# Beta folded into the decay matrix of a gated DeltaNet, and two row scalings issued on ScalarE

## The chip, the core and the metric

The kernel runs on one NeuronCore of one Trainium2 chip. TensorE (PE) does matmuls and transposes, VectorE (DVE), ScalarE (ACT) and GpSimd (POOL) do everything elementwise, SyncE (SP) issues the DMAs. Each engine works through its own queue in the order in which the program was laid out, and waits on semaphores for the others. The metric is the device time of one execution, in microseconds (us), as the median of several runs.

## The reference

One layer of a hybrid encoder on 1024 tokens of width 1024: RMSNorm, an input projection, a causal pooling group and a gated DeltaNet group (4 heads of width 128), an output projection, a squared-ReLU MLP of width 4096 and a last RMSNorm. The change touches the gated DeltaNet only. Its chunked form, cut to what matters here:

```python
qh = l2_norm(heads(q)) * (Dh ** -0.5)
kh = l2_norm(heads(k))
beta = per_head(jax.nn.sigmoid(b.astype(f32)))
gcum = jnp.cumsum(per_head(g), axis=-1)
diff = gcum[..., :, None] - gcum[..., None, :]
decay_incl = jnp.exp(jnp.where(incl, diff, -jnp.inf))
decay_strict = jnp.where(strict, decay_incl, 0.0)
kb = kh * beta[..., None]
m = jnp.einsum('bhncd,bhnjd->bhncj', kb, kh) * decay_strict
sol = lax.linalg.triangular_solve(jnp.eye(C) + m, rhs, left_side=True, lower=True)
attn_inner = jnp.einsum('bhncd,bhnjd->bhncj', qh, kh) * decay_incl
...
o = o * lax.rsqrt(jnp.mean(o * o, axis=-1, keepdims=True) + EPS) * gdn_norm
```

## The kernel before

The program is one straight line of instructions for a sequence cut into two halves of 512 tokens. The kernel works on DeltaNet chunks of 128 tokens, so there are eight chunks (c = 0 to 7), four to a half, and all four heads of a chunk lie side by side in one tile of 128 partitions by 4 x 128 columns.

**Two kinds of work are interleaved on PE.** The dense work is the generator `dense` (L801): the input projections k, q, v, z, p of half 0, then k, q, v, p, z of half 1, then the output projection. Every dense product is three matmuls of 128x512 (a high and a low part of each operand, in the 32-bit replicated format), so every weight tile is first split by ACT (`A.copy(hi, raw)`, L132) and then by DVE or POOL (L133). Between the dense matmuls run the strands: `prepares`, `queries`, `inverts`, `corrects`, `scans` (L692 to L724), each a loop over the eight chunks that waits for flags of the others.

**The order on PE is written out by hand.** A class `Clocked` adds up a nominal time for every matmul, a strand that yields a number sleeps for so much of that nominal time (`SLACK` is 2.0 us, `KHOP` 8.0 us), and `run` weaves the strands into the dense matmuls by it. The diff changes no matmul, no transpose and no yield, and the nominal time counts matmuls and yields alone. The order of ACT, DVE and POOL is not written by hand: the framework's scheduler lays it out with its own estimate of the times, and may pull an instruction ahead as soon as its inputs and its buffer are free in that estimate.

**One chunk**, in the order of its data:

- `prepare` (L515): ACT writes `rh` and `rl`, the triangle `upto` times the high and low part of the gate, a head at a time (L521, four instructions each). PE forms their cumulative differences in `pd`, and the chunk's transposed keys in `pk`. ACT takes `dec = Exp(pd)` (L529), POOL masks it with `upto` (L530) and subtracts the identity to get `ds` (L532). ACT squares `pk` with a sum per row (`squares`, L507, line 510), DVE adds the epsilon (L535), POOL raises to the power -0.5 (`rsqrt`, L152), and DVE scales the keys with that, `kn` (L538). PE transposes `kn`, ACT copies the result to `knT` (L543), POOL makes `kd` (L545), PE multiplies keys by keys into `pm`, and DVE forms `m` from `pm`, `beta` and `ds` in four instructions, one a head (L551). `m` is split into two half-precision tiles `m1`, `m2` (L553 to L555).
- `query` (L559): PE multiplies keys by queries into `pa`, DVE forms `at` from `pa`, `beta` and `dec` in four instructions (L571).
- `invert` (L578): six levels of products on PE. In each, DVE makes `xx` (L595), and ACT copies the two results to `t` and `tt` (L601, L602); the next level's matmuls need all three. `correct` (L608) refines the inverse; DVE makes `ee` (L617) and `hh` (L622) there.
- `scan` (L639): the state recurrence. At its end ACT squares the output, DVE adds, POOL takes the power -0.5 of `so`, and DVE scales the output, `on` (L682). PE transposes `on`, ACT scales it into `qT` (L687), and POOL gates it with `zT` (`gate_out`, L759) for the output projection.

The strand that prepares chunk c+1 starts when chunk c is queried and chunk c-1 scanned, so that preparing, inverting and scanning of neighbouring chunks overlap. Beside the strands DVE carries the causal convolution of q, k, v (three `cy` instructions a tile, L396), the running sums of the pooling group (`nxt`, L414 and L415) and part of the weight splits; ACT carries the copies out of PSUM for both.

Constants (`ident`, `upto`, `low_t`, the level masks) are made once near the start (L229 to L267). `gt` (L493) gives a tile from the pool `gp`, under a name and with a number of buffers; the tiles `rh` and `ds` share one buffer.

Of the kernel before, what the change touches and what calls it, by code (L numbers as in the profile page):

```python
# [8 lines left out]
F32 = mybir.dt.float32  # L9
F32R = mybir.dt.float32r  # L10
F16 = mybir.dt.float16
AF = mybir.ActivationFunctionType
ALU = mybir.AluOpType
PSUM = bass.MemoryType.PSUM

P = 128
# [5 lines left out]
NH = 4  # L22
# [6 lines left out]
def hybrid_trunk(ctx, tc, x, norm_mix, w_in, conv_w, w_pool, pool_scale, a_log, dt_bias,  # L29
                 gdn_norm, w_out, norm_mlp, w_up, w_down, norm_final, out):  # L30
    nc = tc.nc
    V, A, G, T = nc.vector, nc.scalar, nc.gpsimd, nc.tensor
# [23 lines left out]
    def opened(**kw):  # L56
        c = tc.tile_pool(**kw)
        return c, c.__enter__()
# [28 lines left out]
    ident = const.tile([P, P], F32, name="ident")  # L87
# [6 lines left out]
    gpc, gp = opened(name="gp", bufs=1, side="right")  # L94
# [20 lines left out]
    def work_bank():  # L115
        return psg.tile([P, HALF], F32, name="bank", tag="bank")
# [33 lines left out]
    def rsqrt(s):  # L150
        n = s.shape[-1]
        last["rsqrt"] = G.tensor_tensor(s, s, mhalf[:, :n], op=ALU.pow)  # L152
# [90 lines left out]

    upto = gp.tile([P, P], F32, name="upto")
    V.tensor_tensor(upto, ones_f, low_t, op=ALU.subtract)
    upto_r = gp.tile([P, P], F32R, name="upto_r")
    V.tensor_copy(upto_r, upto)

# [2 lines left out]
    for l in range(7):  # L251
        b = 1 << l
        m = gp.tile([P, P], F16, name=f"lev{l}")
# [30 lines left out]
    def done(name, after=0.0):  # L284
        flags[name] = T.now + after
# [198 lines left out]
    def bc(m):  # L484
        return m.unsqueeze(1).broadcast_to(hs)

    def bcol(m):
        return m.unsqueeze(2).broadcast_to(hs)

    def flat(m):  # L490
        return m.rearrange("p h c -> p (h c)")

    def gt(nm, bufs=1, dt=F32, shape=hs, tag=None):  # L493
        return gp.tile(shape, dt, name=nm, tag=tag or nm, bufs=bufs)

    def bank():
        return work_bank().rearrange("p (h c) -> p h c", h=NH)

    def mm(acc, lhsT, rhs, start=True, stop=True):
        for h in range(NH):  # L500
            T.matmul(acc[:, h, :], lhsT[:, h, :], rhs[:, h, :], start=start, stop=stop)

    def tr(acc, src):
        for h in range(NH):
            T.transpose(acc[:, h, :], src[:, h, :], ident)

    def squares(src, acc):  # L507
        junk = gt("junk", dt=F16, shape=[P, P])
        for h in range(NH):
            A.activation(junk, src[:, h, :], AF.Square, accum_out=acc[:, h:h + 1])  # L510

    def of_half(m, c):
        return m[c // CH][:, :, (c % CH) * P:(c % CH + 1) * P]

    def prepare(c, r):  # L515

        g_hi, g_lo, beta, kds, egl, eg, neg = (m[:, c % CH, :] for m in gts[c // CH])
        rh, rl = gt("rh", dt=F32R), gt("rl", dt=F32R)
        for dst, gg in ((rh, g_hi), (rl, g_lo)):
            for h in range(NH):  # L520
                A.activation(dst[:, h, :], upto, AF.Copy, scale=gg[:, h:h + 1].bitcast(F32))  # L521
        yield 2.0 * SLACK
        pd, pk = bank(), bank()
        T.matmul(pd, u_r, flat(rh), start=True, stop=False)
        T.matmul(pd, u_r, flat(rl), start=False, stop=True)
        tr(pk, of_half(kT, c))

        dec = gt("dec")
        A.activation(dec, pd, AF.Exp)  # L529
        G.tensor_tensor(dec, dec, bc(upto), op=ALU.mult)  # L530
        ds = gt("ds", tag="rh")
        G.tensor_tensor(ds, dec, bc(ident), op=ALU.subtract)  # L532
        rk = gt("rk", 2, shape=[P, NH])
        squares(pk, rk)
        V.tensor_scalar(rk, rk, 4 * EPS, None, op0=ALU.add)  # L535
        rsqrt(rk)
        kn = gt("kn")
        V.tensor_tensor(kn, pk, bcol(rk), op=ALU.mult)  # L538
        yield KHOP
        pn = bank()  # L540
        tr(pn, kn)
        knT = gt("knT", 2)
        A.copy(knT, pn)  # L543
        kd = gt("kd", 2)
        G.tensor_tensor(kd, kn, bcol(kds), op=ALU.mult)  # L545
        yield 1.2 * SLACK
        pm = bank()
        mm(pm, knT, knT)
        m = gt("m")
        for h in range(NH):  # L550
            V.scalar_tensor_tensor(m[:, h, :], pm[:, h, :], beta[:, h:h + 1], ds[:, h, :], op0=ALU.mult, op1=ALU.mult)  # L551
        m1, m2 = gt("m1", 2, F16), gt("m2", 2, F16)
        V.tensor_copy(m1, m)  # L553
        G.tensor_tensor(m2, m, m1, op=ALU.subtract)
        V.tensor_tensor(m1, m1, bc(ident_h), op=ALU.add)  # L555
        r.update(m1=m1, m2=m2, kd=kd, egl=egl, beta=beta, knT=knT, dec=dec, eg=eg, neg=neg)
        done(f"prepared{c}", 2.5 * SLACK)

    def query(c, r):  # L559

        qc = of_half(qT, c)
        sq = gt("sq")
        A.activation(sq, qc, AF.Square)
        yield 1.0 * SLACK
        pa, ps = bank(), work_bank()
        mm(pa, r["knT"], qc)
        for h in range(NH):
            T.matmul(ps[:, h:h + 1], sq[:, h, :], ones_c, start=True, stop=True)
        at = gt("at", 2)
        for h in range(NH):  # L570
            V.scalar_tensor_tensor(at[:, h, :], pa[:, h, :], r["beta"][:, h:h + 1], r["dec"][:, h, :], op0=ALU.mult,  # L571
                                   op1=ALU.mult)
        qe = gt("qe", 3, shape=[P, NH])
        V.tensor_scalar(qe, ps[:, 0:NH], 4 * EPS, EPS * P, op0=ALU.add, op1=ALU.mult)
        r.update(qe=qe, at=at)
        done(f"queried{c}")
# [62 lines left out]
    def scan(c, r):  # L639
        old = state[0]  # L640
        w = r["v"]
        if old is not None:
            pw = bank()
            mm(pw, r["knT"], old)
            w = gt("w")
            for h in range(NH):
                V.scalar_tensor_tensor(w[:, h, :], pw[:, h, :], r["neg"][:, h:h + 1], r["v"][:, h, :], op0=ALU.mult,
                                       op1=ALU.add)
            yield 1.2 * SLACK
        py = bank()  # L650
        mm(py, r["ti"], w)
        y = gt("y")
        A.copy(y, py)
        yield 1.0 * SLACK
        if c < NT - 1:
            pst = bank()
            mm(pst, r["kd"], y)
            new = gt("s", 2)
            if old is None:
                V.tensor_copy(new, pst)  # L660
            else:
                for h in range(NH):
                    V.scalar_tensor_tensor(new[:, h, :], old[:, h, :], r["egl"][:, h:h + 1], pst[:, h, :], op0=ALU.mult,
                                           op1=ALU.add)
            state[0] = new
        po = bank()
        mm(po, r["at"], y)
        if old is not None:

            pq, on = bank(), gt("on", tag="w")  # L670
            mm(pq, of_half(qT, c), old)
            A.copy(on, po)
            for h in range(NH):
                V.scalar_tensor_tensor(on[:, h, :], pq[:, h, :], r["eg"][:, h:h + 1], on[:, h, :], op0=ALU.mult,
                                       op1=ALU.add)
            po = on
        so = gt("so", shape=[P, NH])
        squares(po, so)
        V.scalar_tensor_tensor(so, so, 1.0 / P, r["qe"], op0=ALU.mult, op1=ALU.add)
        rsqrt(so)  # L680
        on = po if old is not None else gt("on", tag="w")
        V.tensor_tensor(on, po, bcol(so), op=ALU.mult)  # L682
        done(f"scan{c}", 1.0)
        yield 4.0 * SLACK
        pt = bank()
        tr(pt, on)
        A.activation(of_half(qT, c), pt, AF.Copy, scale=gnorm)  # L687
        done(f"o{c}", 1.5)
# [3 lines left out]
    def prepares():  # L692
        for c in range(NT):
            if c % CH == 0:
                yield f"k{c // CH}"
                yield f"gates{c // CH}"
            if c:
                yield f"queried{c - 1}"
            if c > 1:
                yield f"scan{c - 2}"  # L700
            yield from prepare(c, made[c])

    def queries():
        for c in range(NT):
            yield f"prepared{c}"
            if c % CH == 0:
                yield f"q{c // CH}"
            yield from query(c, made[c])
# [11 lines left out]
    def scans():  # L720
        for c in range(NT):
            yield f"corrected{c}"
            yield f"queried{c}"
            yield from scan(c, made[c])  # L724
# [133 lines left out]
    ub = [P, 4, HALF]  # L858
# [332 lines left out]
```

## Time and profile before

| what | value |
|---|---|
| median of 3 runs | 1155.54 us (1153.03 to 1156.3) |
| time of the profiled execution | 1154.56 us |
| its span, first to last instruction | 1152.9 us |
| mean granted PE clock in the span | 0.987 |

The span is 1.66 us shorter than the time of its own execution; the rest lies around it. Before about 60 us the kernel loads and normalizes the first half and projects its first keys. From there to about 475 us projections and DeltaNet chunks share the engines. After that the MLP runs, in which none of the changed lines occurs. A row of a group reads: line, engine, operation, out<-in, shapes, count, then busy time in us and mean duration of one in ns, then the idle time of that engine just before these instructions and what ended it.

### The profile page before, as it was taken

Reading aid. Unit: us, or ns where it says so; the run is one execution under the profiler, and the core shown is the slowest. Engines: PE = TensorE matmul, PEld = TensorE weight load, DVE = VectorE, ACT = ScalarE, POOL = GpSimd, SP = SyncE. Lnnn points to the kernel's source line nnn. Section 1 sums busy time; section 2 is a strip of 40 time slices with the busy share of each in tenths; the row PEclk is TensorE's granted clock in tenths of the full one; section 3 lists DMA queues with packets and bytes.
Section 4 is the critical chain, followed back from the end, with each engine's and each line's share of the span. In section 5 each row is a group of like instructions: output and inputs, shape, how many; then the busy total and the mean of one; then the engine's idle time right before and its main releaser. Section 6 shows DMA issues by size and latency. Waiting matters only on the chain.

```text
span 1152.9 us, 15516 instructions
## 1 busy us (share of the span) xinstructions
PE 1094.7 (95%) x5606; PEld 890.2 (77%) x5606; DVE 760.5 (66%) x1216; ACT 601.5 (52%) x1117; POOL 267.3 (23%) x247
## 2 busy tenths in 40 slices
PE   6999999989999899977999999999899999999997
PEld 5787887768778788755788888888778888888886
DVE  5797598777887665679655555555455687466584
ACT  6667566666566363654554545454443343334353
POOL 7023144264451200054222222222000000000010
PEclk9999999999999899997999999999989999999999
DMA  5233211111223221130544343434397896365561
GB/s 163 83 111 110 74 53 50 46 55 47 71 64 130 73 84 54 33 104 2 192 145 156 137 164 130 172 122 144 108 389 264 300 380 210 108 194 191 193 209 73
DMA packets 93047, 155.23 MB, mean 135 GB/s; under 512 B 7781, under 2 KB 45738, under 8 KB 92970
## 3 DMA queue, kind: packets, MB, share of 16 engines
q1 hardware_dynamic: 92970, 154.24, 39.6%
q8 instruction: 44, 0.72, 0.3%
q14 instruction: 33, 0.27, 0.1%
HBM read 120.66 MB, written 33.55 MB: 134 GB/s over the span
## 4 chain that ended last, share of the span: by engine, by line
PE 73%; DVE 9%; ACT 3%; POOL 2%; issue 2%; DMA 1%; POOLq 0%; DVEq 0%; SPq 0%; ACTq 0%
PE bank L44 54%; PE acc L44 18%; DVE cy L396 2%; DVE tl L930 1%; PE bank L48 1%; POOL rk L152 1%; DVE xx L595 0%; DMA x<-hd 0%; ACT th L172 0%; DVE r L921 0%; POOL wl L133 0%; DVE nxt L415 0%; DVE wl L936 0%; DVE m L551 0%; POOL wu L955 0%
## 5 line engine op out<-in xcount | busy, mean ns | idle before, releaser
L44 PE MATMUL bank<-th,wh 128*128 128x512 f32 x448 | 178.2, 398 | 11.5 <-ACT th L929 10.5
L44 PE MATMUL bank<-tl,wh 128*128 128x512 f32 x448 | 178.1, 397 | 2.5 <-DVE tl L930 2.4
L44 PE MATMUL bank<-th,wl 128*128 128x512 f32 x448 | 177.6, 396 | 2.2 <-DVE wl L936 2.2
L935 ACT CAST sh<-x 128x1024 fp32r<-128x1024 f32 x55 | 57.9, 1054 | 159.9 <-PE bank L44 153.8
L44 PE MATMUL bank<-th,sh 128*128 128x512 f32 x344 | 133.8, 389 | 0.0
L44 PE MATMUL bank<-th,sl 128*128 128x512 f32 x344 | 133.8, 389 | 0.0
L44 PE MATMUL bank<-tl,sh 128*128 128x512 f32 x344 | 133.8, 389 | 0.0
L44 PE MATMUL acc<-uh,wh 128*128 128x512 f32 x320 | 129.7, 405 | 1.6 <-DVE ul L173 0.9
L935 ACT CAST wh<-wu 128x512 fp32r<-128x512 f32 x112 | 69.1, 620 | 115.4 <-PE bank L44 97.8
L44 PE MATMUL acc<-ul,wh 128*128 128x512 f32 x320 | 128.5, 402 | 0.0
L44 PE MATMUL acc<-uh,wl 128*128 128x512 f32 x320 | 128.1, 400 | 0.0
L936 DVE TENSOR_TENSOR sl<-x,sh 128x1024 fp32r<-128x1024 f32 x55 | 67.3, 1223 | 87.5 <-ACT sh L935 87.5
L936 DVE TENSOR_TENSOR wl<-wu,wh 128x512 fp32r<-128x512 f32 x112 | 81.3, 729 | 45.0 <-ACT wh L935 45.0
L44 PEld LDWEIGHTS bank<-th,wh 128*128 128x128 f32 x448 | 85.1, 190 | 31.8 <-ACT th L929 11.2
L44 PEld LDWEIGHTS bank<-tl,wh 128*128 128x128 f32 x448 | 84.9, 190 | 24.3 <-DVE tl L930 5.2
L44 PEld LDWEIGHTS bank<-th,wl 128*128 128x128 f32 x448 | 85.1, 190 | 22.3 <-DVE wl L936 3.1
L133 POOL TENSOR_TENSOR wl<-raw,wh 128x512 fp32r<-128x512 f32 x48 | 66.9, 1397 | 93.0 <-ACT wh L132 88.7
L152 POOL TENSOR_TENSOR stf<-stf,mhalf 128x1 f32<-128x1 f32 x8 | 7.9, 998 | 329.1 <-DVE stf L1128 329.1
L44 PEld LDWEIGHTS bank<-th,sl 128*128 128x128 f32 x344 | 64.6, 188 | 13.5
L44 PEld LDWEIGHTS bank<-tl,sh 128*128 128x128 f32 x344 | 64.6, 188 | 13.5
L44 PEld LDWEIGHTS bank<-th,sh 128*128 128x128 f32 x344 | 64.5, 188 | 13.3
L44 PEld LDWEIGHTS acc<-uh,wh 128*128 128x128 f32 x320 | 60.3, 188 | 13.6 <-ACT cy L394 1.9
(322 smaller groups left out, 2290.2 us busy)
## 6 DMA issues: line engine op xcount, KB each, us to landing
w<-in_w_down_dram SPq DMA_DIRECT2D x72, 512.0 KB, 6.3
x<-hd SPq DMA_DIRECT2D x56, 512.0 KB, 3.3
raw<-in_w_in_dram SPq DMA_DIRECT2D x80, 256.0 KB, 2.7
wu<-in_w_up_dram SPq DMA_DIRECT2D x16, 1024.0 KB, 5.4
hd<-s SPq DMA_DIRECT2D x48, 256.0 KB, 2.0
hd<-u SPq DMA_DIRECT2D x32, 256.0 KB, 2.1
raw<-in_w_out_dram SPq DMA_DIRECT2D x24, 256.0 KB, 2.5
xin<-in_x_dram SPq DMA_DIRECT2D x8, 512.0 KB, 4.9
```

Source lines behind the costliest of these rows:

```text
L44: T0.matmul(out, lhsT, rhs, start=start, stop=stop, skip_group_check=goes_on)
L48: T0.transpose(out, in_, identity)
L133: eng.tensor_tensor(lo, raw, hi.bitcast(F32), op=ALU.subtract)
L152: last["rsqrt"] = G.tensor_tensor(s, s, mhalf[:, :n], op=ALU.pow)
L396: V.scalar_tensor_tensor(cy, cr[:, e:e + HALF], tap[e], cy, op0=ALU.mult, op1=ALU.add)
L930: V.tensor_tensor(TL[i][:, j, :], block(r, j), TH[i][:, j, :].bitcast(F32), op=ALU.subtract)
L935: A.copy(hi, src)
L936: V.tensor_tensor(lo, src, hi.bitcast(F32), op=ALU.subtract)
```

## The change

The DeltaNet's `beta` is multiplied into the decay matrix itself. For this ACT writes a third tile `ub`, the triangle `upto` times `beta`, a head at a time like `rh` and `rl`. POOL multiplies `dec` by `ub` where it multiplied it by `upto`, and gets `ds` by multiplying with a new constant `above` (the triangle without its diagonal, made once by DVE) where it subtracted the identity. `m` and `at` then need no `beta`: each is one DVE instruction over all heads where it was four. And the two scalings by a row's reciprocal norm, `kn` and `on`, move from DVE (one instruction over all heads) to ACT (four, one a head).

```diff
     V.tensor_tensor(upto, ones_f, low_t, op=ALU.subtract)
+    above = gp.tile([P, P], F32, name="above")
+    V.tensor_tensor(above, upto, ident, op=ALU.subtract)
...
         rh, rl = gt("rh", dt=F32R), gt("rl", dt=F32R)
-        for dst, gg in ((rh, g_hi), (rl, g_lo)):
+        ub = gt("ub")
+        for dst, gg in ((rh, g_hi), (rl, g_lo), (ub, beta)):
             for h in range(NH):
-                A.activation(dst[:, h, :], upto, AF.Copy, scale=gg[:, h:h + 1].bitcast(F32))
+                sc = gg[:, h:h + 1]
+                A.activation(dst[:, h, :], upto, AF.Copy, scale=sc if dst is ub else sc.bitcast(F32))
...
         A.activation(dec, pd, AF.Exp)
-        G.tensor_tensor(dec, dec, bc(upto), op=ALU.mult)
+        G.tensor_tensor(dec, dec, ub, op=ALU.mult)
         ds = gt("ds", tag="rh")
-        G.tensor_tensor(ds, dec, bc(ident), op=ALU.subtract)
+        G.tensor_tensor(ds, dec, bc(above), op=ALU.mult)
...
         kn = gt("kn")
-        V.tensor_tensor(kn, pk, bcol(rk), op=ALU.mult)
+        for h in range(NH):
+            A.activation(kn[:, h, :], pk[:, h, :], AF.Copy, scale=rk[:, h:h + 1])
...
         m = gt("m")
-        for h in range(NH):
-            V.scalar_tensor_tensor(m[:, h, :], pm[:, h, :], beta[:, h:h + 1], ds[:, h, :], op0=ALU.mult, op1=ALU.mult)
+        V.tensor_tensor(m, pm, ds, op=ALU.mult)
...
         at = gt("at", 2)
-        for h in range(NH):
-            V.scalar_tensor_tensor(at[:, h, :], pa[:, h, :], r["beta"][:, h:h + 1], r["dec"][:, h, :], op0=ALU.mult,
-                                   op1=ALU.mult)
+        V.tensor_tensor(at, pa, r["dec"], op=ALU.mult)
...
         on = po if old is not None else gt("on", tag="w")
-        V.tensor_tensor(on, po, bcol(so), op=ALU.mult)
+        for h in range(NH):
+            A.activation(on[:, h, :], po[:, h, :], AF.Copy, scale=so[:, h:h + 1])
```

More of the change, by code (lines that the diff above doesn't have):

```diff
@@ L555, in prepare @@
         V.tensor_tensor(m1, m1, bc(ident_h), op=ALU.add)
-        r.update(m1=m1, m2=m2, kd=kd, egl=egl, beta=beta, knT=knT, dec=dec, eg=eg, neg=neg)
+        r.update(m1=m1, m2=m2, kd=kd, egl=egl, knT=knT, dec=dec, eg=eg, neg=neg)
         done(f"prepared{c}", 2.5 * SLACK)
```

## The prediction

> **What bounds the kernel now.** I read first the page, then the busy times in stretches, then PE's waits.
>
> ```profile
> PE 1094.7 (95%) x5606; PEld 890.2 (77%) x5606; DVE 760.5 (66%) x1216; ACT 601.5 (52%) x1117; POOL 267.3 (23%) x247
> ```
>
> PE is busy for 95% of the span. The change touches no PE instruction, so all it can do is to shorten or lengthen PE's waits, and only where chunks are worked on:
>
> ```profile
> 60.00:384.00 324.00, 308.12 (x2031) 250.11 (x2030) 254.98 (x508) 210.92 (x495) 126.69 (x95) 1.00 0.26 76
> ...
> 375.00:400.00 25.00, 21.97 (x123) 16.60 (x122) 16.66 (x27) 9.77 (x22) 7.53 (x6) 0.86 0.23 79
> ```
>
> The columns after the length are PE, PEld, DVE, ACT and POOL busy time, then the granted clock. In the 324 us of the chunks PE idles 324 - 308.1 = 15.9 us; that is the whole prize. DVE is busy 255.0/324 = 79%, ACT 210.9/324 = 65%. The second row has the one place in there where the clock was held back: (1 - 0.86) x 25 = 3.5 us. Who ends PE's waits in the same 324 us (total, times, longest):
>
> ```profile
> PE bank L44 <- DVE xx L595: 3.3, 6, 0.8
> PE acc L44 <- DVE wol L133: 3.0, 2, 1.9
> PE bank L48 <- DVE kn L538: 2.7, 2, 1.4
> PE bank L44 <- DVE ee L617: 1.6, 2, 0.9
> ...
> PE bank L44 <- ACT qT L397: 1.5, 1, 1.5
> ```
>
> DVE ends most of them. So it looks right to take work off DVE; but the 2.7 us for `kn` end on an operation that the change makes longer.
>
> **The change part by part.** First the prices:
>
> ```profile
> L551 DVE SCALAR_TENSOR_TENSOR m<-bank,beta,ds 128x128 f32<-128x128 f32 x32 | 9.1, 343 | 1.7 <-PE bank L44 1.7
> ...
> L521 ACT ACTIVATE rl<-upto,g_lo 128x128 fp32r<-128x128 f32 x28 | 9.0, 405 | 0.0
> L682 DVE TENSOR_TENSOR on<-on,so 128x512 f32<-128x512 f32 x7 | 7.0, 1001 | 4.2 <-POOL so L152 4.1
> L538 DVE TENSOR_TENSOR kn<-bank,rk 128x512 f32<-128x512 f32 x8 | 5.5, 691 | 7.7 <-POOL rk L152 7.6
> ...
> L571 DVE SCALAR_TENSOR_TENSOR at<-bank,beta,dec 128x128 f32<-128x128 f32 x32 | 9.0, 342 | 2.2 <-PE bank L44 2.2
> ```
> ```profile
> 251.12 1.13 DVE L551 SCALAR_TENSOR_TENSOR m<-bank,beta,ds 128x128 f32<-128x128 f32 x4 [1.18 <-PE bank L44]
> ```
> ```profile
> 280.69 1.28 ACT L521 ACTIVATE rl<-upto,g_lo 128x128 fp32r<-128x128 f32 x4
> ```
>
> Small instructions overlap in their queue: four of `m` take 1.13 us, not 4 x 0.343. One over all heads, with one operand in PSUM, has the price of `kn`, 0.69. So **`m` and `at`** give DVE 0.44 us each a chunk, not the 0.68 that the means suggest. **`kn` and `on`** give 0.69 each. Per chunk 2.26, in eight chunks 18 us, or 5 to 6 points of DVE's 79%. DVE also stood idle 7.6 us ahead of `kn` and 4.1 us ahead of `on`, waiting for POOL's power with other work queued behind; these waits move to ACT.
>
> ACT gets three groups of four a chunk (**`ub`, `kn`, `on`**), 1.28 each by the row of `rl`, which has the same form: a 128x128 tile with a scale from a column. That is 3.84 a chunk, 31 us in all, and ACT goes from 65% to about 74%. Reading PSUM as `kn` does could be cheaper or dearer; I keep 1.28.
>
> POOL's two products keep their shape and I take their price as unchanged. `ub` must be there before POOL multiplies, and its one buffer is free again only when POOL is done with the chunk before; it is needed a chunk later, so it costs ACT time only. The constant `above` has the price of `upto`, a DVE instruction of the same shape that runs once:
>
> ```profile
> L245 DVE TENSOR_TENSOR upto<-ones_f,low_t x1: 391/391/391, 26.3 to 26.3; 128x128 f32<-128x128 f32 x1
> ```
>
> It costs 0 to 0.39 us; I take 0, since PE then has a full projection queued. Neither SP's queue nor a DMA is touched.
>
> **What PE gains.** A wait shrinks where DVE ran without a pause from a removed instruction up to the one that PE waited for.
>
> ```profile
> 332.70 0.69 DVE L538 TENSOR_TENSOR kn<-bank,rk 128x512 f32<-128x512 f32 x1 [0.90 <-POOL rk L152]
> ```
> ```profile
> 336.75 0.38 PE L44 MATMUL bank<-xx,tt 128*128 128x128 f16 x4 [0.42 <-DVE xx L595]
> ...
> 343.08 0.38 PE L44 MATMUL bank<-xx,tt 128*128 128x128 f16 x4 [0.81 <-DVE xx L595]
> ```
>
> From 332.70 to the second `xx` DVE works without a pause. Without `kn` it starts 0.90 + 0.69 = 1.59 us earlier, more than both waits: 0.42 + 0.81 = **1.23**.
>
> ```profile
> 233.43 0.69 DVE L682 TENSOR_TENSOR on<-on,so 128x512 f32<-128x512 f32 x1 [1.12 <-POOL so L152]
> ```
> ```profile
> 232.22 0.69 ACT L394 ACTIVATE cy<-acc,cols 128x512 f32<-128x512 f32 x1
> ```
> ```profile
> 238.82 0.38 PE L44 MATMUL bank<-xx,tt 128*128 128x128 f16 x4 [1.49 <-ACT qT L397]
> ```
>
> The convolution behind `on` starts as that ends, at 234.1 less the overlap of the queue; its input left ACT at 232.91. It can go about 1.1 us earlier, and `xx` and `qT` with it: **1.1** of the 1.49.
>
> ```profile
> 146.09 0.69 DVE L538 TENSOR_TENSOR kn<-bank,rk 128x512 f32<-128x512 f32 x1
> ```
> ```profile
> 149.56 0.38 PE L44 MATMUL bank<-xx,tt 128*128 128x128 f16 x4 [0.39 <-DVE xx L595]
> ...
> 87.13 0.38 PE L44 MATMUL bank<-xx,tt 128*128 128x128 f16 x4 [0.84 <-DVE xx L595]
> ...
> 304.28 0.40 PE L44 MATMUL bank<-tt,ee 128*128 128x128 f16 x4 [0.79 <-DVE ee L617]
> ```
>
> The first lies behind a `kn`: **0.39**. The other two lie behind `at` and `m`, with 0.44 to gain: **0.88**. Sum of the gains 1.23 + 1.1 + 0.39 + 0.88 = 3.6.
>
> **What PE loses.**
>
> ```profile
> 245.89 0.69 DVE L538 TENSOR_TENSOR kn<-bank,rk 128x512 f32<-128x512 f32 x1 [0.69 <-POOL rk L152]
> ```
> ```profile
> 246.07 0.58 ACT L601 CAST t<-bank 128x512 f16<-128x512 f32 x1
> 246.54 0.59 ACT L602 CAST tt<-bank 128x512 f16<-128x512 f32 x1
> ```
> ```profile
> 246.73 0.41 PE L48 MATMUL bank<-ident,kn 128*128 128x128 f32 x2 [1.45 <-DVE kn L538]
> ...
> 291.63 0.41 PE L48 MATMUL bank<-ident,kn 128*128 128x128 f32 x2 [1.28 <-DVE kn L538]
> ```
>
> In chunk 4 ACT is free for `kn` at 246.07 at the earliest, so it ends at 247.35 in place of 246.58 (0.8 later); behind `t` and `tt` it ends at 248.3 (1.75 later). I take **1.2**. In chunk 5 it is late by 1.28 - 0.69 = **0.6**. The other six `kn` and seven `on` had no wait of PE behind them.
>
> ```profile
> 281.03 1.77 DVE L682 TENSOR_TENSOR on<-on,so 128x512 f32<-128x512 f32 x1
> ```
> ```profile
> 282.95 0.30 PE L48 MATMUL bank<-ident,on 128*128 128x128 f32 x1 [0.41 <-DVE on L682]
> ```
>
> Here `on` would stand behind the four `rl` above (280.69 + 1.28 = 281.97) and end at 283.25 in place of 282.80, **0.5** later; ahead of them it would be 0.4 earlier. I keep the order of the trace.
>
> ```profile
> 369.82 0.62 ACT L132 CAST wh<-raw 128x512 fp32r<-128x512 f32 x1 [0.60 <-PE acc L44]
> 370.92 0.59 ACT L601 CAST t<-bank 128x512 f16<-128x512 f32 x1 [0.48 <-PE bank L44]
> ```
>
> An `on` of 1.28 at 369.4 fills the rest of the first gap (0.4) and the second (0.48); ACT, busy without a pause after that, is **0.4** late, and with it the split weights that PE waits for at 380.5. Last, the copies `t` and `tt` of the inversion, in the same queue, can be caught behind a group that waits for POOL. Such a hit costs the group, 1.28, and the mean wait for POOL, (7.6 + 4.1)/16 = 0.73, less the slack of the copy:
>
> ```profile
> 252.88 0.61 ACT L602 CAST tt<-bank 128x512 f16<-128x512 f32 x1
> ```
> ```profile
> 254.20 0.62 PE L44 MATMUL bank<-t,m 128*128 128x128 f16 x8
> ```
>
> 254.20 - 253.49 = 0.71, so 1.3 a hit. How often it happens the trace of before can't show, since the order of ACT is laid out anew: from none to sixteen. I count one hit, **1.3**, because PE waited for a `kn` or an `on` only three times in sixteen, so these groups mostly fall where PE has other work queued. Sum of the losses 1.2 + 0.6 + 0.5 + 0.4 + 1.3 = 4.0.
>
> **Sum.** +4.0 - 3.6 = +0.4 us on the profiled execution: 1154.56 + 0.4 = 1154.9. That execution was 1.0 below the median of 1155.54, so for the median I say **1155.9 us**: no change. What a measurement can tell here is about 0.3%, 3.5 us.
>
> [...] If all sixteen moved groups lay in PE's way, 16 x 0.59 would make it 1155.5 + 9.4 = 1164.9; the waits show three of sixteen that do.
>
> **Rivals.**
>
> *ACT becomes the queue that holds PE* (slower). `kn` and `on` sit in ACT's queue at their place and wait there for POOL's power; behind them `t` and `tt` are held, which PE needs at every level of the inversion. At 1.3 a hit it decides from four hits on, three more than I count (1155.9 + 3.9 = 1159.8); six give 1155.9 + 6.5 = **1162.4**. For it: the waits ahead of `kn` were seen on DVE, six times in eight. Against it: ACT pauses for 324 - 210.9 = 113 us of the stretch, so most groups find it free. [...]
>
> *The splits at 375 to 383 come free* (faster).
>
> ```profile
> 375.27 3.44 POOL L759 TENSOR_TENSOR qT<-qT,zT 128x512 f32<-128x512 f32 x2
> ```
> ```profile
> 377.48 2.38 DVE L767 TENSOR_TENSOR ml<-pT,mh 128x512 fp32r<-128x512 f32 x2
> ```
> ```profile
> 380.51 0.50 PE L44 MATMUL acc<-wol,mh 128*128 128x512 f32 x1 [1.93 <-DVE wol L133]
> ```
>
> DVE's `ml` lasts until POOL's gating ends, the third `wol` waits behind it, and the clock is held back just after. If the new order of the queues parts these, both waits (3.0) and the clock's loss (3.5) go: 1155.9 - 6.5 = **1149.4**. For it: the scheduler lays out all three queues anew. Against it: no changed instruction stands between them, and ACT feeds them later, not earlier. [...]
>
> *DVE's relief reaches PE more often than the trace shows*: `xx`, `ee` and `qT` together are 6.4 us, of which I count 3.6. Alone this gives 1155.9 - 2.8 = 1153.1, inside my forecast's band.
>
> **How the numbers follow.** No change 0.52; ACT holds PE 0.24; the splits come free, or DVE's relief adds to part of it, 0.24. The range goes from 1148.0 (a little below the second rival) to 1162.4 (the first); about one in ten is left out on either side. Faster by over 0.3% 0.24, within it 0.52, slower 0.24.
>
> **What would show it.** In the profile after: four ACT instructions of `kn` that take about 1.28 together; DVE near 73% and ACT near 74% in the stretch of the chunks; no wait of PE at the two `xx` after 336; PE's waits on `kn` grown from 2.7 to about 4.5 and under ACT's name; at most one or two on `t` more than before. I am wrong if PE's idle time there differs by more than 3.5 us from 15.9, or if the clock's loss near 380 is gone.

## The result, and the profile after

| kernel | median, us | runs | ratio to before (95% interval) |
|---|---|---|---|
| before | 1155.92 | 4 | |
| after | 1163.16 (1162.8 to 1164.28) | 4 | 1.0069 (1.0051 to 1.0088) |

The change makes the kernel 7.2 us slower. The forecast was no change, 1155.9, and the range ended at 1162.4. The nearest rival was "ACT becomes the queue that holds PE", by its time and by its engine; its mechanism was another one. The four runs of the changed kernel had a mean granted clock of 0.980 to 0.983, and the 81 runs of the kernel before that the experiments are compared with 0.984 to 0.988 (one run of 3859 us is left out of the ratios).

The first part of the page after, and the busy times in stretches (columns as before: PE, PEld, DVE, ACT, POOL, granted clock):

```profile
PE 1102.0 (95%) x5606; PEld 894.7 (77%) x5606; DVE 741.8 (64%) x1153; ACT 626.5 (54%) x1213; POOL 263.9 (23%) x247
```
```profile
60.00:384.00 324.00, 310.03 (x2018) 251.21 (x2017) 232.52 (x443) 228.56 (x569) 120.91 (x93) 0.98 0.25 74
375.00:400.00 25.00, 21.92 (x123) 16.70 (x122) 14.82 (x20) 15.14 (x40) 9.21 (x8) 0.86 0.32 106
```

The work moved much as was said: DVE lost 760.5 - 741.8 = 18.7 us (18 forecast) and stands at 72% in the chunks, ACT got 25 us (31 forecast) and stands at 70.5%. PE even idles less in the 324 us: 14.0 us where it was 15.9. But it also did less: 2018 matmuls where there were 2031, at a clock of 0.98 where it was 1.00. So the loss is not idle time of PE alone, and the view that the prediction watched for it (idle off by 3.5 us) does not see it. Who ended PE's waits between 60 and 480 us (total, times, longest):

```profile
PE bank L48 <- ACT kn L544: 6.8, 4, 3.0
PE acc L44 <- DVE wol L133: 3.0, 2, 1.9
PE bank L44 <- ACT t L604: 2.6, 4, 1.1
PE bank L44 <- DVE xx L598: 1.4, 4, 0.5
```

`xx` fell from 3.3 to 1.4, as hoped. `kn` rose from 2.7 to 6.8, and the two long ones are these, in chunk 4 and in chunk 6:

```profile
247.98 1.25 PE L48 MATMUL bank<-ident,kn 128*128 128x128 f32 x4 [2.69 <-ACT kn L544]
```
```profile
340.62 1.25 PE L48 MATMUL bank<-ident,kn 128*128 128x128 f32 x4 [2.99 <-ACT kn L544]
```

The order of PE's instructions is the same in both kernels, so the start of the same instruction can be compared between the two traces. At 236 us of the trace of before PE is 0.3 us late, at 240 it is 1.3 early, at 256 2.8 late (chunk 4: +4.1), from 291 to 335 1.7 late, at 352 5.9 late (chunk 6: +4.1); from there to 480 it stays (6.2), and the MLP adds 2.3 more. Each of the two steps is larger than the wait that stands in it, 1.23 and 2.99 us more than before. Most of the rest is the clock. The stretches around the two waits, two for chunk 4 and three for chunk 6:

```profile
244.33:247.74 3.41, 0.90 (x9) 0.58 (x8) 2.12 (x5) 2.19 (x5) 2.51 (x3) 1.00 0.54 151
247.74:251.16 3.42, 3.18 (x9) 2.47 (x10) 0.00 (x0) 1.55 (x5) 1.41 (x2) 0.50 0.27 77
...
336.49:339.91 3.42, 1.14 (x5) 0.58 (x4) 3.42 (x8) 1.23 (x4) 2.65 (x2) 1.00 0.47 118
339.91:343.32 3.41, 2.70 (x14) 2.32 (x15) 3.03 (x6) 2.56 (x7) 1.33 (x2) 0.50 0.10 36
343.32:346.73 3.41, 3.41 (x9) 2.38 (x8) 0.00 (x0) 0.76 (x2) 0.61 (x1) 0.50 0.01 2
```

Behind the wait in chunk 4 PE runs 3.4 us at half clock, behind that in chunk 6 6.8 us; by the starts of the same matmuls 1.6 and 2.4 us are lost in them. Not all of that is the clock: PE starts the four transposes of `kn` 0.26 us apart there, as ACT hands over the heads one by one, where they were 0.11 apart, and that is about 0.5 us in each chunk; the same step costs 0.5 us in chunk 5, at full clock. The trace of before has no such spell between 60 and 381 us.

**Why `kn` came late.** ACT around chunk 6, before:

```profile
328.43 0.28 ACT L510 ACTIVATE junk<-bank 128x128 f16<-128x128 f32 x1
328.59 0.21 ACT L510 ACTIVATION_READ_ACCUMULATOR junk<-bank 128x1 f32 x1
328.83 0.28 ACT L510 ACTIVATE junk<-bank 128x128 f16<-128x128 f32 x1
...
329.23 0.28 ACT L510 ACTIVATE junk<-bank 128x128 f16<-128x128 f32 x1
...
329.63 0.28 ACT L510 ACTIVATE junk<-bank 128x128 f16<-128x128 f32 x1
```

and after:

```profile
331.36 0.27 ACT L512 ACTIVATE junk<-bank 128x128 f16<-128x128 f32 x1
...
332.64 0.30 ACT L512 ACTIVATE junk<-bank 128x128 f16<-128x128 f32 x1
...
332.91 1.29 ACT L525 ACTIVATE ub<-upto,beta 128x128 f32<-128x128 f32 x4
334.08 0.63 ACT L132 CAST wh<-raw 128x512 fp32r<-128x512 f32 x1
334.59 0.61 ACT L604 CAST t<-bank 128x512 f16<-128x512 f32 x1
335.06 0.61 ACT L605 CAST tt<-bank 128x512 f16<-128x512 f32 x1
335.54 0.32 ACT L512 ACTIVATE junk<-bank 128x128 f16<-128x128 f32 x1
...
336.79 0.33 ACT L512 ACTIVATE junk<-bank 128x128 f16<-128x128 f32 x1
...
340.20 1.14 ACT L544 ACTIVATE kn<-bank,rk 128x128 f32<-128x128 f32 x4 [2.47 <-POOL rk L152]
```

The four squares that give the norm of the keys used to go out 0.40 us apart. Now they are spread over 5.4 us, with the new `ub` and other work between them. They all write the one buffer `junk`, which nobody reads; each waits for the one ahead of it to be out of it (in the kernel before, the second starts at 328.83 and the read of the first sum ends at 328.80), and in its place the scheduler puts whatever of ACT is ready. The last square of chunk 6 starts 2.95 us behind the transposes into `pk` before, and 8.36 behind them after; DVE's epsilon, POOL's power and `kn` follow it. ACT itself stood idle 2.47 us for that power.

Chunk 4 is a mixed case. Its squares were spread over 6.6 us already before (235.93 to 242.52), and the last one starts 9.29 us behind the transposes in place of 8.29. And there `kn` does stand behind `t` and `tt` in ACT's queue, as the prediction had it; the power was done at 246.88:

```profile
245.87 1.01 POOL L152 TENSOR_TENSOR rk<-rk,mhalf 128x4 f32<-128x4 f32 x1 [0.90 <-DVE rk L540]
```
```profile
247.07 0.59 ACT L605 CAST tt<-bank 128x512 f16<-128x512 f32 x1
247.55 1.16 ACT L544 ACTIVATE kn<-bank,rk 128x128 f32<-128x128 f32 x4
```

### The profile page after: what moved, and what is told of

It is laid out like the page before. It is cut to its first block, busy times and chain, and to the rows that moved or that the text cites. A ratio compares the mean times of both kernels' runs of the same rounds, so it can differ in the third digit from the quotient of the medians.

```text
span 1161.3 us, 15546 instructions
## 1 busy us (share of the span) xinstructions
PE 1102.0 (95%) x5606; PEld 894.7 (77%) x5606; DVE 741.8 (64%) x1153; ACT 626.5 (54%) x1213; POOL 263.9 (23%) x247
## 4 chain that ended last, share of the span: by engine, by line
PE 73%; DVE 7%; ACT 6%; issue 2%; POOL 1%; DMA 1%; POOLq 0%; DVEq 0%; SPq 0%; ACTq 0%
PE bank L44 54%; PE acc L44 18%; DVE cy L398 2%; PE bank L48 1%; DVE tl L934 1%; ACT wh L132 0%; DMA x<-hd 0%; ACT t L604 0%; ACT th L172 0%; DVE r L925 0%; ACT junk L512 0%; ACT on L686 0%; ACT rl L525 0%; DVE wol L133 0%; DVE nxt L417 0%
## 5 line engine op out<-in xcount | busy, mean ns | idle before, releaser
L398 DVE SCALAR_TENSOR_TENSOR cy<-cr,cols,cy 128x512 f32<-128x512 f32 x72 | 66.5, 928 | 10.7 <-ACT cy L396 10.0
```

The source lines that it names most:

```text
L398: V.scalar_tensor_tensor(cy, cr[:, e:e + HALF], tap[e], cy, op0=ALU.mult, op1=ALU.add)
```

## The experiments

Three theories. **S**: the added groups on ACT spread the squares over the one `junk` buffer; the power, and so `kn`, is late. **K** (the prediction's own account of chunk 4): `kn` is late because its own scaling now stands in ACT's queue. **L**: ACT simply has too much to do. All ratios are to runs of the kernel before on the same chip, with 95% intervals.

**Which part loses.** Four kernels put parts of the change back.

e1: the changed kernel with `kn` on DVE again.

```diff
-        for h in range(NH):
-            A.activation(kn[:, h, :], pk[:, h, :], AF.Copy, scale=rk[:, h:h + 1])
+        V.tensor_tensor(kn, pk, bcol(rk), op=ALU.mult)
```

> The changed kernel with kn scaled by DVE again; ub, on, m and at stay changed. Theory S (the added ACT groups ub and on stand among the squares of pk, so the power rk comes late, whoever scales kn): the last square stays 1 to 5 us later after the transposes of pk than before (it was 2.0 to 8.3 us before, 3.2 to 9.3 after), PE still waits 4 us or more for kn, and the time stays at 1160 to 1165 us. Theory K (the scaling of kn in ACT's queue is itself the loss): the waits on kn go back to 2.7 us or less, the time to 1153 to 1157 us.

Measured: 1161.73 us, 1.0048 (1.0034 to 1.0063). Most of the loss stays, and so do PE's waits, now under DVE's name:

```profile
PE bank L48 <- DVE kn L543: 8.5, 5, 3.4
```

K falls as the main cause: the squares of chunk 6 are as late as in the changed kernel (8.35 us behind the transposes), and PE's wait there is 3.4 us in place of 3.0. In chunk 4 the wait is 2.46 us in place of 2.69; so little hung on ACT's queue ahead of `kn`.

e2: the changed kernel with `on` on DVE again (the same edit in `scan`). e3: both again on DVE, so that only the folded `beta` is left. e4: the other way round, the kernel before with `kn` and `on` on ACT and no fold.

> The changed kernel with on scaled by DVE again; ub and kn stay on ACT. Theory S: one of the two groups that stand among or ahead of the squares is gone, so about half of the loss of 7 us goes: 1157 to 1161 us, the last square about 1.3 us earlier than in the changed kernel where on stood ahead of it. Theory K: no change, 1161 to 1165 us.

> Only the fold of beta (ub on ACT, m and at one instruction each); kn and on on DVE as before. Theory S: ub alone among the squares, a part of the loss stays: 1156 to 1161 us. Theory K: no loss, and DVE's relief of 0.9 us a chunk shows: 1152 to 1156 us.

> The kernel before with kn and on scaled by ACT; no ub, beta stays in m and at. Theory S: on alone ahead of the squares, about half of the loss: 1157 to 1161 us. Theory K: the whole loss, 1161 to 1165 us, with PE waiting 6 us or more for kn.

| | median, us | ratio | last square of chunk 6 behind `pk`, us | wait for `kn` there, us |
|---|---|---|---|---|
| e2 | 1158.83 | 1.0027 (1.0017 to 1.0036) | 5.49 | 1.06 |
| e3 | 1161.37 | 1.0044 (1.0028 to 1.0059) | 5.44 | 3.33 |
| e4 | 1165.37 | 1.0084 (1.0070 to 1.0098) | 7.46 | 3.97 |

e2 came out where S expected it, e3 0.4 us above. e4 did not: its time lies just above the range of K, and its waits for `kn` of 7.3 us in all are what K expected. But its trace does not show K's mechanism in chunk 6, where `kn` starts 0.03 us behind the power. There DVE, busy with the pooling group's `nxt`, gives the epsilon only 3.6 us behind the start of the last square (0.4 in the kernel before, 1.8 in the changed one). That adds to the late squares and is not part of S.

No part is innocent: each of them that adds groups to ACT moves the squares of chunk 6 from 2.95 to 5.4 us or more. But the squares are not all of it. In e2 and e3 the power of chunk 6 ends at 337.10 and 337.21 us, and `kn` starts at 337.13 on ACT and at 339.16 on DVE, behind a `nxt` of the pooling group: 2 us of e3's wait are DVE's queue, and there the scaling on ACT is the better one. The parts do not add up either: 0.44% for the fold and 0.84% for the scalings, 0.69% for both. The order of the queues is laid out anew in each kernel.

**Taking the cause away.** e5: the changed kernel, with four buffers for the squares' output. No work is removed.

```diff
-        junk = gt("junk", dt=F16, shape=[P, P])
         for h in range(NH):
+            junk = gt("junk", 4, F16, [P, P])
             A.activation(junk, src[:, h, :], AF.Square, accum_out=acc[:, h:h + 1])
```

> The changed kernel with four buffers for junk, the tile that the squares write and nobody reads. With one buffer each square must wait for the one ahead of it, and the scheduler puts one other ACT instruction or group (t, wh, ub, on) between any two; with four the squares of a chunk stand together in ACT's queue. Nothing else is changed and no work is taken away. Theory S (the gaps between the squares fill with the added ACT groups, so the power and kn come late): the last square comes within 4 us of the transposes in every chunk (3.2 to 9.3 us in the changed kernel), PE's waits on kn fall from 6.8 to under 1.5 us, the half-clock spells near 248 and 340 us are gone, and the time falls to 1150 to 1156 us. Theory L (31 us more ACT work cost what they cost, in whatever order): 1160 to 1165 us.

Measured: 1156.18 us, 1.0008 (0.9999 to 1.0017). The squares of chunk 6 in its timeline are together again, and closer than before, 0.25 us apart:

```profile
326.93 0.26 ACT L512 ACTIVATE junk<-bank 128x128 f16<-128x128 f32 x1
...
327.18 0.27 ACT L512 ACTIVATE junk<-bank 128x128 f16<-128x128 f32 x1
...
327.43 0.28 ACT L512 ACTIVATE junk<-bank 128x128 f16<-128x128 f32 x1
...
327.68 0.29 ACT L512 ACTIVATE junk<-bank 128x128 f16<-128x128 f32 x1
```

No wait for `kn` is left in the list of PE's waits, and no spell at half clock before 379 us. In the stretch from 60 to 384 us ACT is busy 230.5 us, not less than the 228.6 of the changed kernel. The time is 0.2 us above the range that S gave. So S holds for the changed kernel and L falls: 7.0 of the 7.2 us hang on one buffer.

Does the change then gain? At 377 us of the trace of before PE is 2.8 us ahead in e5. That is no proof of the prediction's gains, since e6 below has a lead of 2.4 us at 324 us without the change (e5 2.7). e5 loses its lead between 377 and 383, where the fourth weight split `wol` comes no earlier than it did:

```profile
PE acc L44 <- DVE wol L133: 4.9, 3, 2.8
```

e6: the kernel before with the same four buffers. e8: the fold alone (e3) with them. e9: the moved scalings alone (e4) with them.

> The kernel before with four buffers for junk. Theory S: it had two late kn of its own (chunks 4 and 5, 2.7 us of PE waits), which go: 1151 to 1155 us. Theory L: no change, 1154 to 1157 us.

> The fold of beta alone (ub on ACT; kn and on on DVE) with four buffers for junk. Theory S: the loss of 5 us that the fold alone showed goes and DVE's relief is left: 1150 to 1155 us. Theory L: 1158 to 1162 us, as with one buffer.

> kn and on on ACT, no fold, with four buffers for junk (with one buffer it took 1165.4 us, the worst of all). Theory S: the squares stand together, the waits on kn go, 1152 to 1157 us. Theory L (ACT's load): 1162 to 1166 us.

Measured: e6 1156.67 us, 1.0006 (0.9997 to 1.0015); e8 1156.81, 1.0008 (0.9998 to 1.0017). Both are above the ranges of S (e6 in that of L) and have no wait for `kn`. e6 gives its lead back at two others; e8 has no lead at 324 us:

```profile
PE bank L44 <- DVE xx L595: 5.3, 5, 2.5
...
PE bank L44 <- DVE nxt L414: 1.8, 1, 1.8
```

e9 was a miss: 1163.73, 1.0050 (1.0033 to 1.0067), where S alone would have it near before. Its waits for `kn` are gone too, but PE waits 2.0 us for `ee`, 1.8 for `nxt` and 5.0 for `wol`, and its clock is half in four places between 180 and 396 us. So S does not explain the loss of the moved scalings alone, and what they displace there is not shown.

e7: the changed kernel with a longer nominal sleep between `kn` and its transposes, to give the late power time.

```diff
-KHOP = 8.0
+KHOP = 11.0
```

> The changed kernel with KHOP 11.0 in place of 8.0: PE's order has 3 us more of other work between the transposes of pk and those of kn. Theory S: PE's waits on kn fall from 6.8 to under 2 us and most of the loss goes, 1153 to 1158 us, though every chunk is strung out by 3 us. Theory L: 1160 to 1165 us.

A miss for S: 1161.34, 1.0045 (1.0032 to 1.0058), which is in the range of L. The wait for `kn` fell to 0.4 us as S said, but each chunk ends later and the inversions now wait, so the run does not decide between the two:

```profile
PE bank L44 <- DVE xx L598: 8.9, 7, 1.9
```

**The place near 380.** The third `wol` (a weight split on DVE) waits for two `ml` of the output projection that are pulled ahead of it; the first runs beside POOL's gating and takes 1.77 us there, the second starts behind it and takes 0.68. e10 puts them behind it, in the changed kernel with four buffers; e11 does so in the kernel before, e12 in e6, e14 in the changed kernel with its one buffer.

```diff
-        eng.tensor_tensor(lo, raw, hi.bitcast(F32), op=ALU.subtract)
+        last["split"] = eng.tensor_tensor(lo, raw, hi.bitcast(F32), op=ALU.subtract)
...
         wt[0] += wout_weights(0, range(4, KT))
+        last["lows"] = last["split"]
...
-    parts = out_split(NT - 1)
+    with tc.issue_after(last["lows"].ins):
+        parts = out_split(NT - 1)
...
-    whole(out_proj(4, 0, wt[0], work_bank))
+    with tc.issue_after(last["lows"].ins):
+        early = out_split(4)
+    whole(out_proj(4, 0, wt[0], work_bank, early))
```

> The changed kernel with four buffers for junk and, besides, the three splits ml of later tokens (tiles 7 and 4) laid behind the four splits wol on DVE, which PE waits for near 375 to 383 us; they stood among them and were held there by POOL's gating. With four buffers alone PE was 2.7 us ahead of the kernel before at 374 us and lost it there. Expected: PE's waits on wol fall from 4.9 to under 1 us and the half-clock spell that follows goes, 1148 to 1152 us. Rival: the weights come late for another reason (ACT's split or the load), no change, 1155 to 1158 us.

> The kernel before with the same order on DVE for wol and ml alone. Expected: the wait of 3.0 us for wol and up to 3.4 us of the clock's loss go, 1149 to 1153 us. Rival: no change, 1154 to 1157 us.

> The kernel before with both (four buffers for junk, the order of wol and ml): the fair comparison for the changed kernel with both. If the change itself is worth something once its two side effects are taken away, this is slower than the changed kernel with both by 1 to 4 us; if the change is worth nothing, the two are within 1 us.

> The changed kernel with its one junk buffer, and the two split parts of the output projection issued on DVE behind the weight splits. That order took 1155.92 - 1149.9 = 6.0 us off the kernel before and 1156.18 - 1150.39 = 5.8 off the changed kernel with four junk buffers. If the late squares of chunks 4 and 6 and the third weight split are two losses that add up: 1163.16 - 5.9 = 1157.3, with the spells at half clock behind kn of chunks 4 and 6 still there and the one near 387 shorter or gone. If they are one loss (the lead lost at 340 decides what is late at 380): 1150 to 1152.

| | median, us | ratio |
|---|---|---|
| e10 | 1150.39 | 0.9952 (0.9940 to 0.9964) |
| e11 | 1149.90 | 0.9947 (0.9935 to 0.9959) |
| e12 | 1152.76 | 0.9970 (0.9959 to 0.9981) |
| e14 | 1160.38 | 1.0031 (1.0017 to 1.0046) |

In e11 the list of PE's waits up to 480 us is that of before to a tenth of a us but for this row (3.0 before), and no spell at half clock is left in that stretch:

```profile
PE acc L44 <- DVE wol L133: 1.8, 2, 1.1
```

That is 6.0 us for the order of a few instructions. At the place itself, between 377 and 390 us, PE gains 3.8 us: 1.2 of the wait and 2.6 of the clock. The profile of e11 gains another 1.9 in the MLP, where the reordered instructions are long past. In e10 the waits for `wol` fell to 2.6 us and not to under 1, and a spell of 3.4 us is left where 6.8 were. Both e10 and e11 beat both kernels, and e11 does it without the change. e10 and e12, which differ by the change alone, are 2.4 us apart, with intervals that just overlap; so much it may be worth once its side effect and this place are out of the way. e12 is 2.9 us behind e11, so the four buffers are no gain in the kernel before. e14 lies above both of its expectations: the loss in the chunks stays, and the order gives 2.8 us by the medians in place of 5.9 (by the ratios 4.4, since the kernel before was 0.8 us slower on that chip). Its profile has no spell near 387; the one in chunk 4 is 6.8 us in place of 3.4 and that in chunk 6 3.4 in place of 6.8. Between 377 and 390 us PE's lag falls by 3.6 us in e14 as it does by 3.8 in e11, so by the traces the two losses are separate. What e14 misses is in the MLP, which takes 2.8 us more in its profile than in that of before.

**Does a late `kn` alone cost so much?** e15, e16 and e17 delay POOL's power of chunk 6 in the kernel before, with three, four and five products into a tile that nobody reads; e18 has two of them, e19 two of half the width.

```diff
         V.tensor_scalar(rk, rk, 4 * EPS, None, op0=ALU.add)
+        if c == 6:
+            hold = gt("hold")
+            for _ in range(3):
+                G.tensor_tensor(hold, bc(upto), bcol(rk), op=ALU.mult)
         rsqrt(rk)
```

> The kernel before, with three products of 128x512 on POOL put ahead of the power of rk in chunk 6 alone, and nothing else. In the profile before, kn of chunk 6 ends at 333.39 and PE takes it at 335.7, so it has 2.3 us to spare; a POOL product there takes about 1.25. Three make 3.75, so PE should wait about 1.4 us for kn. Theory T (a wait of PE below about 1.5 us leaves the clock alone): no spell at half clock within 15 us behind it, and the time grows by the wait or less, 1155.9 + 1.4 = 1157.3 at most. Rival (what costs is the spread of the squares or the added ACT work, not the wait): 1156 to 1157.3 too. Rival (any wait of PE brings a spell): 3.4 us at half clock behind it, 1155.9 + 1.4 + 1.7 = 1159.0.

> As above with four products: 5.0 us, PE should wait about 2.7 us for kn of chunk 6. Theory T (a wait of 1.8 us or more brings on a spell at half clock, whoever caused it): a spell of 3.4 or 6.8 us within 10 us behind the wait, 1.7 or 3.4 us lost, so 1155.9 + 2.7 + 1.7 to 3.4 = 1160.3 to 1162.0. Rival (the wait costs itself alone; the clock falls for another reason in the changed kernel): no new spell, 1158.6 at most.

> As above with five products: 6.25 us, PE should wait about 3.9 us for kn of chunk 6. Theory T: a spell as with four products, of 6.8 us rather than 3.4, 1155.9 + 3.9 + 3.4 = 1163.2. Rival (the wait costs itself alone): no new spell, 1159.8 at most.

> The kernel before with two products of 128x512 on POOL ahead of the power of rk in chunk 6 alone. With three of them the two first took 3.13 us and a weight split of 1.82 followed them ahead of the power, so here the power starts 3.13 + 1.82 = 4.95 us later at most; less the 2.3 that kn has to spare PE waits some 2.7 us, about as long as in the changed kernel (2.99). Theory T (the wait itself brings on the half clock): a spell of 6.8 us within 10 us behind it, 1155.9 + 2.7 + 3.4 = 1162.0, less what PE's later waits give back. Rival (the changed kernel's spell needs its ACT work or its spread squares): no spell behind it, 1158.6 at most.

> As above, with two products of half the width (128x256): about 1.6 us instead of 3.13, so kn is 3.4 us later and PE waits some 1.1 us. Theory T with a threshold between 1.45 and 1.8 us: no spell behind it, 1157.0 at most. Without a threshold: a spell of 3.4 us, 1155.9 + 1.1 + 1.7 = 1158.7.

| | PE's wait for `kn`, us | half clock within it or just behind it, us | median, us | ratio |
|---|---|---|---|---|
| e19 | 1.85 | none | 1156.67 | 1.0006 (0.9996 to 1.0016) |
| e18 | 2.70 | none | 1158.17 | 1.0017 (1.0008 to 1.0027) |
| e15 | 6.06 | 6.8 | 1163.96 | 1.0066 (1.0050 to 1.0081) |
| e16 | 7.71 | 10.2 | 1164.28 | 1.0066 (1.0048 to 1.0084) |
| e17 | 9.15 | 10.2 | 1164.88 | 1.0067 (1.0046 to 1.0088) |

The first three doses were too large: POOL's weight splits got in between the products. They do show that one late power in one chunk, with nothing else edited, can cost as much as the whole change (7.2 to 8.2 us over the 1156.73 of before on that chip), and that a longer wait costs little more. e18 has the dose of the changed kernel and refutes the theory as it was put, that a wait of 1.8 us or more brings on the half clock: 2.70 us brought none, 2.69 in chunk 4 of the changed kernel did.

```profile
341.39 0.63 PE L48 MATMUL bank<-ident,kn 128*128 128x128 f32 x4 [2.70 <-DVE kn L542]
```

What tells these two apart is where the wait lies. In every profile the spells at half clock start on one grid of 3.41 us. Two windows of e18's grid, found by counting 3.4133 us back from its spell at 387.9:

```profile
336.74:340.15 3.41, 1.95 (x9) 1.27 (x8) 3.38 (x6) 0.71 (x2) 3.41 (x3) 1.00 0.05 7
340.15:343.57 3.42, 2.17 (x18) 1.98 (x19) 3.42 (x5) 1.51 (x3) 3.07 (x3) 1.00 0.38 110
```

A line of the grid cuts e18's wait in two: PE is busy 1.95 and 2.17 us of the two windows, and the clock stays. In chunk 4 of the changed kernel, shown above, the wait lies almost whole in one window, which has 0.90 us of work, and the next window runs at half clock.

## Why the prediction was wrong

**The step that failed** stands under "What PE loses": "The other six `kn` and seven `on` had no wait of PE behind them." It costed `kn` from the end of POOL's power and took the time of that power as given, and so looked only at chunks where PE already waited for `kn`. But the power hangs on the squares, the squares are on ACT, and the change adds twelve instructions a chunk to ACT's queue, some of which landed between them. Chunk 6 had 2.3 us to spare in the trace of before and was left out; it lost 5.4 us in the squares. e1 and e5 show it: with the scaling back on DVE most of the loss stays, with the squares in four buffers it goes. Chunk 0 is another of the six: its last square comes 6.27 us behind the transposes in place of 4.35, PE waits 0.32 us for `kn`, and it falls back by 1.0 us there.

**What was missing from the sum** is what follows a wait, the clock above all. The waits of chunks 4 and 6 grew by 1.23 + 2.99 = 4.2 us, and PE fell behind by 4.1 + 4.1 = 8.2 there. The slower matmuls behind the two waits make 1.6 + 2.4 = 4.0 of it, about 1.0 of this by the heads that come one by one. Small new waits in chunk 4 (+1.4, where PE was early by what it had won at 238.82) and small old ones that went in chunk 6 (-1.3) cancel.

The other terms, by how much PE's lag behind the trace of before changes from the instruction ahead to the one named:

| step of the prediction | forecast, us | PE's change at that place, us |
|---|---|---|
| gain: 87.13 and 304.28 (behind `at` and `m`) | 0.88 | 0.99 + 0.24 |
| gain: 149.56 (`xx` behind `kn`) | 0.39 | 0.50 |
| gain: 238.82 (convolution behind `on`) | 1.1 | 1.65 |
| gain: 336.75 and 343.08 (`xx` behind `kn`) | 1.23 | 0.43 + 0.97 |
| loss: `kn` of chunk 4 | 1.2 | 1.25, and the clock behind it |
| loss: `kn` of chunk 5 | 0.6 | -0.52 at the first transpose, -0.05 behind the fourth |
| loss: `on` of chunk 3 at 282.95 | 0.5 | -0.57, a gain |
| loss: ACT late at 369 to 380 | 0.4 | 0.17 |
| loss: one hit on `t` or `tt` | 1.3 | 1.0 (`t` from 1.6 to 2.6) |

The gains were read rightly in place and nearly in size; at 238.82 all of the wait went. But three of them might have gone in any case: PE came 3.6 and 5.6 us later to those at 336 and 343, and 1.0 later to the one at 87.13, by what `kn` of chunk 0 had cost it. What was gained up to 225 us was lost again at 229, where PE, being early, waited 1.09 us in place of 0.33 for a `t` that ACT gave at its old time; that is most of the 1.0 in the last row, and no hit by a moved group. PE's waits for `t` in the trace of before:

```profile
PE bank L44 <- ACT t L601: 1.6, 3, 1.0
```

The loss at 282.95 had the wrong sign, and the one at chunk 5 did not come. `kn` of chunk 5 shows why: on DVE one instruction gave all four heads, on ACT PE starts at the first of four, so a scaling that ends later can release PE earlier (the first head ends at 293.29, PE starts at 293.34, and the last head ends at 294.07). The four transposes then take 1.10 us where they took 0.63, since the heads come one by one, and the gain is spent.

```profile
293.34 1.10 PE L48 MATMUL bank<-ident,kn 128*128 128x128 f32 x4 [0.75 <-ACT kn L544]
```

The prices held. Four of `kn` take 1.14 to 1.19 us and four of `ub` 1.27 to 1.33, for which 1.28 was taken:

```profile
L544 ACT ACTIVATE kn<-bank,rk 128x128 f32<-128x128 f32 x32 | 9.2, 378 | 3.9 <-POOL rk L152 3.9
```

Of the marks that were to show it, those for DVE and `xx` came true; ACT came to 70.5% in place of 74. `kn` went to 6.8 in place of 4.5, and the clock's loss near 380 stayed (0.86 in both). Neither of the two signs of being wrong appeared: both looked where the loss was not.

**The rivals.** "ACT becomes the queue that holds PE" had the right engine and nearly the right time, but not the mechanism: it let `kn` and `on` hold `t` and `tt`. PE's total on `t` grew by 1.0 us alone. What ACT's queue held in chunk 6 was the chain ahead of `kn`; in chunk 4 the power came 1.0 us later, and then `t` and `tt` held `kn` by another 0.7, the reverse of what the rival had. So it was partly luck that its 1162.4 came near. "The splits at 375 to 383 come free" did not happen in the changed kernel. e11 parted the same instructions by hand and gained 6.0 us where 6.5 was worked out, but not by the same terms: of the waits 1.2 us went in place of 3.0, of the clock's loss 2.6 in place of 3.5, and the rest came in the MLP.

**What stays open.** Why e9 loses with its squares together, and so whether moving `kn` and `on` has a price that the buffer of the squares does not explain. The 2.3 us that the MLP adds in the profiled execution of the changed kernel hardly belong to the change: e15, in which no changed line occurs, adds 2.3 there as well, and of the 18 other profiles with the same order on PE all but that of e11 take 0.3 to 2.8 us more there than the profile of before, which was a lucky one there. And nobody chose where on the grid a wait fell: the counts below are read from the profiles, not set by a run.

## What to carry to other kernels

Before work is added to an engine's queue, look at the sequences on that engine that others wait for, not only at the instructions that are moved: count what the slowest of them has to spare, in every chunk and not just where PE already waits. A scratch output that nobody reads should have as many buffers as the sequence has instructions, since one buffer lets a scheduler pull the sequence apart; here that is worth 7 us in the changed kernel and nothing in the kernel before. And where PE is 95% busy, price a wait by what the clock does after it too: the 3 us of chunk 6 cost 5.4 until the next waits gave some of it back.

## What the runs showed of the hardware

**The spells at half clock start on one grid in each profile.** In each of the twenty profiles, the starts of all spells at half clock behind 60 us lie on one grid with a pitch of 3.4133 us (within 0.005 us in the two of before and after), and the spells last 3.41, 6.83, 10.24 or 13.65 us (the one that runs past the end apart). Its place against the kernel's start differs between profiles (the spell near 380 starts at 381.65 us before and at 387.69 after, 6.04 us apart, which is no multiple of the pitch). Counting PE's idle time by its records in each window of that grid between 60 and 500 us, over the twenty profiles: 34 windows at full clock had 1.82 us of idle or more, and all 34 were followed by half clock; 14 had 1.46 to 1.80 us, and 3 of them were; 2474 had less, and none was. At half clock, all 20 windows that were idle for over a fifth were followed by another at half clock, and of 38 with less, one was. The window ahead of the loss near 380 in the kernel before, and its two followers:

```profile
378.24:381.65 3.41, 1.48 (x9) 0.67 (x7) 3.02 (x6) 1.72 (x4) 1.50 (x2) 1.00 0.28 82
381.65:385.07 3.42, 2.33 (x6) 1.82 (x6) 3.31 (x6) 1.14 (x2) 1.76 (x2) 0.50 0.44 156
385.07:388.48 3.41, 3.41 (x17) 2.85 (x17) 0.99 (x2) 1.37 (x3) 0.00 (x0) 0.50 0.24 73
```

The first is idle 1.93 us of 3.41, all in the one wait for the third `wol`; the wait of 1.09 lies in the second, which stays at half clock. So the clock's loss there came with the first wait; in e11, where the longest wait for `wol` is 1.1 us, no spell follows.

A little over half a window of idle time was enough in these profiles (1.82 of 3.41 us), in two pieces too (0.73 and 1.09 us in e10), and the wait of 2.70 us in e18 that a line of the grid cut in two cost no clock.

**The squares with a sum** of chunk 6 start 0.25 us apart in e5, where each has its own output, and 0.40 us apart in the kernel before, where they share one, though their busy times are nearly the same (0.26 to 0.29 us, and 0.19 to 0.22 us for the read of the sum, which overlaps its square).
